# Hybrid encoder step: fewer and later kept weight pairs, norm stages apart, and other buffers and turns for column stores and loads

## The chip, the core and the metric

The kernel runs on one core of a Trainium2 chip. The metric is the device time in microseconds of one execution. Of the kernel before there are three such times: 2317.66, 2319.67 and 2321.96, median 2319.67. One further execution was profiled; every duration below is from it.

## The reference

One layer of a streaming encoder in float32, for 2048 prompt tokens and 32 sample tokens of width 1024:

```python
h = layer_norm(x, ln_in_g, ln_in_b)
z = einsum('btd,de->bte', h, w_in)              # 1024 -> 2304
ax, ag, bq, bk, bv, bg, cq, ck, cv = split(z)
o_a = rg_lru(causal_conv(ax)) * gelu(ag)        # A, 4 channel groups
o_b = head_norm(retention(bq, bk, bv)) * silu(bg)   # B, 4 heads
o_c = sliding_window_attention(cq, ck, cv)      # C, 8 query heads, 2 kv heads
m = einsum('bte,ed->btd', concat(o_a, o_b, o_c), w_out)
h = layer_norm(ALPHA * h + m, ln1_g, ln1_b)
f = einsum('btf,fd->btd', silu(h @ w_gate) * (h @ w_up), w_down)   # hidden width 2816
y = layer_norm(ALPHA * h + f, ln2_g, ln2_b)
```

Besides y, the new states of the three mixers are returned. float32 accuracy is reached with three matmuls for one product: weight and activation are each split into a high part (fp32r) and the rest, and high x high, rest x high and high x rest are added up.

## The kernel before

**Two halves.** The first half of the program takes the prompt in six blocks of 256, 384, 384, 384, 384 and 256 tokens; the 32 sample tokens go with block 0. It does LN, input projection, mixers, output projection and LN1 of all blocks, and the SwiGLU of block 0 in between. The second half, from 1093 us to the end, does the SwiGLU of the other 1792 tokens with combined (Strassen-like) products; its lines are 1330 and higher. The change is nearly all in the first half.

**Units.** The first half is a list of units, one for each weight tile of 0.5 MB. W units (18 in a block, f = 0 to 17) are the input projection, 24 matmuls each (L908, through `product`); O units (8 in a block) the output projection; G units (44, two for each f of 0 to 21) gate and up of block 0; D units its down projection. They run in this order: W of block 0, W of block 1, O of block 0, W of block 2, O of block 1, and so on to O of block 4; then G and D of block 0 up to f = 11, O of block 5 (the last), and G and D to f = 21. In the profiled execution, W of block 1 begins at about 105 us, W of the last block at about 701, and G at about 816.

**A unit's weights.** `feed` issues the load of a raw tile on SP's queue (L245, three `stage` buffers). `split` makes the pair from it: ScalarE writes the high part (L250), VectorE the rest (L254). The `pair` buffers are three. A unit that `keeps` names also stores its pair to DRAM (L261, two DMAs of 512 KB, in `keptW` or `keptO`); in later blocks `known` is true, and the finished pair (1 MB) is loaded (L238) with no split. Units of odd x are kept in block 1, those of even x in block 2.

**What sets the order.** The program writes the order of every engine's instructions out itself. Ahead of each unit's matmuls come `feed`, `split`, `run_late` (actions that were put off by one unit) and `step`. `step` is one turn: it advances side work written as generators. Those in `express` go on by a fixed number of yields; the others take turns while `pace["credit"]` lasts, which grows with the unit's time and falls by the cost that each yield names. `wait(n)` yields for n turns. An engine works through its instructions in order, so an instruction that waits holds up all behind it on its engine, and an engine's DMA queue likewise.

**Side work that the change touches.**
- `norm` (n for LN, m for LN1 of a block): per row tile the statistics (L372 to L374), then two passes (L380, L382) on VectorE; `pipeline` runs the tiles a stage apart. One norm at a time: its name stands in the list `norming`.
- `gained` (g0): multiplies block 0's three row tiles by the LN gain and adds its offset (six passes, L398) in block 1's W units. It puts "g0" into `norming` too.
- `mix_b` (B): retention in chunks; L716 to L725 states and statistics, L731 normalises into `b_o`, L737 transposes it on TensorE, L739 writes it out.
- `to_memory` (in m): TensorE transposes the LN1 output (L429), ScalarE copies it from PSUM to one of three `stg` buffers (L431) and stores it from its own queue to DRAM (L433 for block 0, L439 for others).
- `columns0` (f0): loads block 0's columns back in three parts (L470) and splits them (L473, L474) for the G units.
- `columns_first` (x0): in the last G units loads the first columns of the second half (L1273, L1277) and makes their sums and splits (L1289 to L1297). It is started by `change`, once m of the last block is drained.
- G units make `g_t` (L964, L965, L972), its high part `hCh` (L973) and the rest `hCl` (L978); D units (`t_unit`, L995 to L1005) add up in PSUM banks taken from the four `mm` banks, and `accumulate` adds these to the rows (L1022, L1026).

Of the kernel before, what the change touches and what calls it, by code (L numbers as in the profile page):

```python
# [97 lines left out]
def tile_hybrid_step(ctx: ExitStack, tc: tile.TileContext, io, outs):  # L98
# [117 lines left out]
    def keeps(u):  # L216

        kind, b, x = plan[u][:3]
        return kind in "WO" and b == 1 + (x % 2 == 0)

    def known(u):

        kind, b, x = plan[u][:3]
        return kind in "WO" and b > 1 + (x % 2 == 0)

    def unit_pair(u):
        pair = fw.tile([128, 2048], F32R, name="pair", bufs=NUNIT)
# [61 lines left out]
    def step():  # L289

        for name, n in list(express.items()):
            for _ in range(n):
                if name in side:
                    advance(name)
        pace["turns"] += 1
        pace["credit"] = min(pace["credit"], pace["most"]) + pace["rate"]
        for name in pace["turn"][:]:
            if pace["credit"] <= 0.0:
                break
            pace["turn"].remove(name)  # L300
            pace["turn"].append(name)
            pace["credit"] -= advance(name)

    def wait(turns):

# [51 lines left out]
    def norm(name, b, g, be):  # L357

        while norming or len(tok.get(b, ())) < len(ttiles(b)) or pace["turns"] < arrived.get(b, 0):
            yield 0.0  # L360
        norming.append(name)
        n = len(ttiles(b))
        gt, bt = bcast(g), bcast(be)
        here = pace["turns"] + 4
        st = sb.tile([128, n, 2, 6], F32, name="ln_st", bufs=2)
        mv = sb.tile([128, n, 2], F32, name="ln_mv", bufs=2)
        rs = sb.tile([128, n], F32, name="ln_rs", bufs=2)

        def tile_(t, rows):
            x = tok[b][t][:rows, :]  # L370
            for i in range(2):
                dve.bn_stats(st[:rows, t, i, :], x[:, i * 512:(i + 1) * 512])  # L372
            dve.bn_aggr(mv[:rows, t, :], st[:rows, t])
            dve.tensor_scalar(rs[:rows, t:t + 1], mv[:rows, t, 1:2], EPS, None, op0=ALU.add)  # L374
            yield 1.75
            pool.tensor_tensor(rs[:rows, t:t + 1], rs[:rows, t:t + 1], mhalf[:rows, 0:1], op=ALU.pow)
            yield 0.1
            while pace["turns"] < here:
                yield 0.0
            dve.scalar_tensor_tensor(x, x, mv[:rows, t, 0:1], gt[:rows, :], op0=ALU.subtract, op1=ALU.mult)  # L380
            yield 1.35
            dve.scalar_tensor_tensor(x, x, rs[:rows, t:t + 1], bt[:rows, :], op0=ALU.mult, op1=ALU.add)  # L382
            yield 1.35

        yield from pipeline([tile_(t, rows) for t, (_, rows) in enumerate(ttiles(b))], 1)
        norming.clear()

    def gained(b):
# [33 lines left out]

    def to_memory(b):

        def half(t, c0, rows, h):
            p = sdbank().rearrange("p (f c) -> p f c", f=4)
            for f in range(4):
                ft = 4 * h + f
                pe.transpose(p[:, f, :rows], tok[b][t][:rows, ft * 128:(ft + 1) * 128], ident[:rows, :rows])  # L429
            stg = sb.tile([128, 4, 128], F32, name="stg", bufs=3)  # L430
            act.activation(stg[:, :, :rows], p[:, :, :rows], AF.Copy)  # L431
            if b == 0:
                act.dma_start(cols0[:, 4 * h:4 * h + 4, c0:c0 + rows], stg[:, :, :rows])  # L433
            else:
                s, off = divmod(START[b] + c0 - START[NBLK], PART)
                for th in range(2):
                    a0, a1 = max(off, th * HALF), min(off + 128, th * HALF + HALF)
                    if a0 < a1:
                        act.dma_start(cols1[s, th, h][:, :, a0 - th * HALF:a1 - th * HALF],  # L439
                                     stg[:, :, a0 - off:a1 - off])  # L440
            yield 0.1

        yield from pipeline([half(t, c0, rows, h) for t, (c0, rows) in enumerate(ttiles(b)) for h in range(2)], 2)
# [20 lines left out]
    def columns0():  # L464

        h, l = hB[0] = hl(0, "hA")
        n = ncol(0)
        for k0, k1 in ((0, 3), (3, 6), (6, 8)):
            w = row_tile()[:, :(k1 - k0) * n].rearrange("p (k c) -> p k c", c=n)
            sp.dma_start(w, cols0[:, k0:k1, :])  # L470
            yield from wait(4)
            for k in range(k0, k1):
                act.activation(h[:, k, :], w[:, k - k0, :], AF.Copy)  # L473
                dve.tensor_tensor(l[:, k, :], w[:, k - k0, :], h[:, k, :].bitcast(F32), op=ALU.subtract)  # L474
                yield 0.5
# [189 lines left out]
    def mix_b(b):  # L665
# [11 lines left out]
        def chunk(c0, n, state, gi):  # L677
# [54 lines left out]
                                  op0=ALU.subtract, op1=ALU.mult)  # L732
            yield 1.4
            yield 0.0
            pt = sdbank().rearrange("p (f c) -> p f c", f=4)
            for i in range(2):
                pe.transpose(pt[:, i, :n], on[:n, 2 * i:2 * i + 2, :].rearrange("p h e -> p (h e)"), ident[:n, :n])  # L737
# [245 lines left out]
    def t_unit(b, key, kts, wh, wl, wf, first, last):  # L983

        tiles = ttiles(b)
        if first:
            banks[key] = [mmbank() for _ in tiles]
        wh, wl, wf = (w if w is None else w.rearrange("p (k c) -> p k c", k=2) for w in (wh, wl, wf))
        for x, (ah, al, _) in enumerate(kts):
            for t, (c0, rows) in enumerate(tiles):  # L990
                if rows < 128:
                    continue
                o = banks[key][t]
                cs = slice(c0, c0 + rows)
                pe.matmul(o, ah[:, cs], wh[:, x, :], start=first and x == 0, stop=False)  # L995
                pe.matmul(o, al[:, cs], wh[:, x, :], start=False, stop=False)  # L996
                pe.matmul(o, ah[:, cs], wl[:, x, :], start=False, stop=last and x == 1)  # L997
            if x == 0 and pace["twice"]:
                step()
        if tiles[-1][1] < 128:  # L1000

            for x, (_, _, a) in enumerate(kts):
                for h in range(2):
                    q = 2 * h + x
                    pe.matmul(banks[key][-1][32 * q:32 * q + 32, 0:256], a, wf[:, x, h * 256:(h + 1) * 256],  # L1005
                              start=first, stop=last)
# [261 lines left out]

    def columns_first():

        a = [two(), two()]
        for k in range(2):
            sp.dma_start(a[k], cols1[0, 0, 0][:, 2 * k:2 * k + 2, :])  # L1273
# [111 lines left out]

    kept_pair = {}

    def new_pair(key):
        at, n = (wp, 3) if clock["made"] % NPAIR < 3 else (sb, NPAIR - 3)
        clock["made"] += 1  # L1390
        pair = at.tile([128, 2, 512], F32R, name="pair", bufs=n)
# [29 lines left out]
    def w_keep(key):  # L1421

        def fn():
            sums[key[1:]] = dr.tile([128, 2, 512], F32, name="sum%d%s" % key[1:])
            sp.dma_start(sums[key[1:]], kept_pair[key].bitcast(F32))
        jobs.append(("store", fn, ()))

    def w_known(key):
# [79 lines left out]

    def background(n):
        clock["slot"] += 1  # L1510
        loads()
        while n and clock["done"] < clock["next"]:
            kind, _, on = jobs[clock["done"]]
# [403 lines left out]
```

## Time and profile before

| | us |
|---|---|
| median of three executions | 2319.67 |
| the profiled execution | 2317.79 |
| its span | 2315.8 |

ScalarE's waits in the first half show where the side work stands in the way of others: L250 waited for `stage` loads 58.7 us in 16 waits (in_wgu), 38.0 in 9 (in_wout) and 33.2 in 12 (in_win), all beside running matmuls but a few. One DMA queue moves 407.35 of the 417.90 MB. The profile is read from the span's start; a row of the timeline has start, duration, engine, line, operation, tiles (out<-in), and in brackets the idle time before it with what ended it.

### The profile page before, as it was taken

The numbers are of one execution on the slowest core, as the hardware profiler recorded it, in microseconds if no ns is written. First come the engines' busy times: TensorE is split into PE (matmuls) and PEld (weight loads), VectorE is DVE, ScalarE is ACT, GpSimd is POOL, SyncE is SP. The second block draws the span as 40 slices with busy tenths as digits, with TensorE's granted clock in tenths as the row PEclk, the third lists the DMA queues.
The fourth block names the chain that finished last, engine by engine and source line by source line (L and its number), as shares of the span: only waits on it lengthen the run. The fifth ranks groups of instructions, "written<-read, shape, count | busy, mean of one in ns | idle before, by whom it ended". The sixth has DMA issues, their size and how long they took to land.

```text
span 2315.8 us, 31921 instructions
## 1 busy us (share of the span) xinstructions
PE 2243.0 (97%) x12168; PEld 1956.8 (84%) x12168; DVE 1479.7 (64%) x2656; ACT 790.6 (34%) x1585; POOL 158.0 (7%) x236
## 2 busy tenths in 40 slices
PE   8999999999999999989999999999999999999996
PEld 7887888988888879877888988888888888898884
DVE  7795757566446375567876766677787544454557
ACT  5646263351523334234322332322331222232221
POOL 2010201101001011010000000000000000000004
PEclk9999999999999999989999999999999999999998
DMA  6563686767758765764643442433556343343341
GB/s 221 177 197 111 233 268 212 273 225 244 265 184 309 263 199 174 254 210 146 248 158 115 159 151 95 168 127 130 203 187 215 122 154 114 110 154 115 132 132 64
DMA packets 139272, 417.90 MB, mean 180 GB/s; under 512 B 20272, under 2 KB 35440, under 8 KB 127472
## 3 DMA queue, kind: packets, MB, share of 16 engines
q1 hardware_dynamic: 119056, 407.35, 51.4%
q10 hardware_dynamic: 20064, 8.52, 1.3%
q8 instruction: 96, 1.57, 0.3%
q14 instruction: 56, 0.46, 0.1%
HBM read 316.55 MB, written 99.26 MB: 180 GB/s over the span
## 4 chain that ended last, share of the span: by engine, by line
PE 25%; issue 22%; DVE 3%; DMA 1%; POOL 0%; ACT 0%; SPq 0%; DVEq 0%; ACTq 0%; POOLq 0%
PE gu L1578 16%; PE mm L1647 3%; PE mm L1646 3%; PE mm L1648 3%; DVE end_st L1713 0%; DVE tok L1711 0%; DVE end_mv L1721 0%; POOL end_rs L1718 0%; DMA pair<-sum3t 0%; DVE pair L1406 0%; DMA out_y<-tok 0%; DVE xl L1330 0%; DVE tok L1733 0%; DMA tok<-rows 0%; DVE tok L1333 0%
## 5 line engine op out<-in xcount | busy, mean ns | idle before, releaser
L1578 PE MATMUL gu<-xh,pair 128*128 128x448 f32 x2464 | 555.4, 367 | 7.1 <-DVE two L1600 2.9
L1578 PEld LDWEIGHTS gu<-xh,pair 128*128 128x128 f32 x2464 | 463.5, 188 | 50.0 <-issue 3.7
L908 PE MATMUL mm<-hAh,pair 128*128 128x384 f32 (+2 forms) x2432 | 424.6, 323 | 16.4 <-DVE pair L254 5.6
L908 PEld LDWEIGHTS mm<-hAh,pair 128*128 128x128 f32 x2432 | 376.6, 192 | 40.9 <-issue 17.7
L1401 ACT ACTIVATE pair<-ww 128x512 fp32r<-128x512 f32 x308 | 189.8, 626 | 515.8 <-PE mm L1648 237.9
L1578 PE MATMUL gu<-xl,pair 128*128 128x448 f32 x1232 | 303.0, 367 | 0.1
L1406 DVE TENSOR_TENSOR pair<-ww,pair 128x512 fp32r<-128x512 f32 x308 | 208.4, 688 | 147.9 <-ACT pair L1401 137.8
L1578 PEld LDWEIGHTS gu<-xl,pair 128*128 128x128 f32 x1232 | 232.1, 189 | 21.4 <-DVE xl L1330 1.1
L1655 DVE TENSOR_TENSOR tok<-tok,mm 128x512 f32<-128x512 f32 x181 | 124.1, 688 | 161.2 <-PE mm L1648 160.2
L1646 PE MATMUL mm<-pair,g 128*128 128x512 f32 x571 | 225.1, 394 | 1.8 <-DVE tok L1653 1.8
L1647 PE MATMUL mm<-pair,g 128*128 128x512 f32 x571 | 225.1, 394 | 0.0
L1648 PE MATMUL mm<-pair,g 128*128 128x512 f32 x571 | 224.6, 393 | 0.0
L908 PE MATMUL mm<-hAl,pair 128*128 128x384 f32 (+2 forms) x1216 | 211.2, 316 | 0.0
L250 ACT ACTIVATE pair<-stage 128x1024 fp32r<-128x1024 f32 x131 | 138.1, 1055 | 189.1 <-DMA stage<-in_wgu 58.7
L908 PEld LDWEIGHTS mm<-hAl,pair 128*128 128x128 f32 x1216 | 192.5, 192 | 0.0
L254 DVE TENSOR_TENSOR pair<-stage,pair 128x1024 fp32r<-128x1024 f32 x130 | 158.2, 1218 | 31.1 <-ACT pair L250 28.7
L1646 PEld LDWEIGHTS mm<-pair,g 128*128 128x128 f32 x571 | 107.3, 188 | 27.1 <-DVE tok L1653 2.3
L1648 PEld LDWEIGHTS mm<-pair,g 128*128 128x128 f32 x571 | 107.4, 188 | 24.9
L1647 PEld LDWEIGHTS mm<-pair,g 128*128 128x128 f32 x571 | 107.3, 188 | 24.3
L995 PE MATMUL mm<-pair,hCh 128*128 128x512 f32 x216 | 91.1, 422 | 7.3 <-DVE tok L1026 4.7
L997 PE MATMUL mm<-pair,hCh 128*128 128x512 f32 x216 | 86.7, 401 | 0.5 <-DVE pair L254 0.4
L996 PE MATMUL mm<-pair,hCl 128*128 128x512 f32 x216 | 86.9, 402 | 0.2 <-DVE hCl L978 0.2
(297 smaller groups left out, 2641.4 us busy)
## 6 DMA issues: line engine op xcount, KB each, us to landing
pair<-keptW SPq DMA_DIRECT2D x63, 1024.0 KB, 5.4
ww<-in_wgu SPq DMA_DIRECT2D x154, 256.0 KB, 3.2
pair<-keptO SPq DMA_DIRECT2D x28, 1024.0 KB, 4.9
stage<-in_win SPq DMA_DIRECT2D x45, 512.0 KB, 4.7
stage<-in_wgu SPq DMA_DIRECT2D x44, 512.0 KB, 4.2
ww<-in_wdn SPq DMA_DIRECT2D x88, 256.0 KB, 3.1
keptW<-pair SPq DMA_DIRECT2D x36, 512.0 KB, 8.0
stage<-in_wdn SPq DMA_DIRECT2D x22, 512.0 KB, 3.8
```

What stands on the lines that cost most here:

```text
L250: act.activation(whi[u], staged[u], AF.Copy)
L254: eng.tensor_tensor(wlo[u], staged[u], whi[u].bitcast(F32), op=ALU.subtract)
L908: pe.matmul(p, w[:, k, :], a[:, k, :], start=(x == 0 and k == 0), stop=(x == 2 and k == 7))
L995: pe.matmul(o, ah[:, cs], wh[:, x, :], start=first and x == 0, stop=False)
L996: pe.matmul(o, al[:, cs], wh[:, x, :], start=False, stop=False)
L1401: act.activation(pairs[key][1], whole_w[x], AF.Copy)
L1406: dve.tensor_tensor(pairs[key][0], whole_w[x], pairs[key][1].bitcast(F32), op=ALU.subtract)
L1578: pe.matmul(bank[n], w[:, k * 128:k * 128 + 128], a[:, k, :], start=first and x == 0 and k == 0, stop=x == 2 and k == 3, skip_group_check= ...
L1646: pe.matmul(bank, gh, wh, start=first and f == fs[0], stop=False)
L1647: pe.matmul(bank, gl, wh, start=False, stop=False)
L1648: pe.matmul(bank, gh, wl, start=False, stop=last and f == fs[-1])
L1655: dve.tensor_tensor(r, r, bank, op=ALU.add)
```

## The change

It does eight things.
1. `keeps`, `known`: odd x are kept in block 1, x%4 = 2 in block 2, x%4 = 0 in block 3; in the last block even x are loaded raw and split again.
2. `norm` runs its pipeline with each stage as a yield of its own, and `step` then goes on with what is in `norming` while credit is left. This holds for g0 as well.
3. `to_memory` of the last block uses halves of row tiles in place of the three `stg` buffers.
4. `columns0` loads one part ahead.
5. `mix_b` has one more yield ahead of its transposes.
6. `t_unit` takes the `gu` banks of the second half for the D units of half 1, once these exist.
7. `columns_first` waits six turns first.
8. The second half's stores of kept sums are put off by one turn.

```diff
--- before.py
+++ after.py
@@ -216,12 +216,14 @@
     def keeps(u):
 
         kind, b, x = plan[u][:3]
-        return kind in "WO" and b == 1 + (x % 2 == 0)
+        return kind in "WO" and b == 1 + (x % 2 == 0) + (x % 4 == 0)
 
     def known(u):
 
         kind, b, x = plan[u][:3]
-        return kind in "WO" and b > 1 + (x % 2 == 0)
+        if b == NBLK - 1 and x % 2 == 0:
+            return False
+        return kind in "WO" and b > 1 + (x % 2 == 0) + (x % 4 == 0)
 
     def unit_pair(u):
         pair = fw.tile([128, 2048], F32R, name="pair", bufs=NUNIT)
@@ -300,6 +302,12 @@
             pace["turn"].remove(name)
             pace["turn"].append(name)
             pace["credit"] -= advance(name)
+        for name in [n for n in pace["turn"] if n in norming]:
+            while name in side and name in norming and pace["credit"] > 0.0:
+                cost = advance(name)
+                pace["credit"] -= cost
+                if cost < 0.5:
+                    break
 
     def wait(turns):
 
@@ -382,7 +390,7 @@
             dve.scalar_tensor_tensor(x, x, rs[:rows, t:t + 1], bt[:rows, :], op0=ALU.mult, op1=ALU.add)
             yield 1.35
 
-        yield from pipeline([tile_(t, rows) for t, (_, rows) in enumerate(ttiles(b))], 1)
+        yield from pipeline([tile_(t, rows) for t, (_, rows) in enumerate(ttiles(b))], 1, True)
         norming.clear()
 
     def gained(b):
@@ -422,12 +430,19 @@
 
     def to_memory(b):
 
+        spare = {}
+
         def half(t, c0, rows, h):
             p = sdbank().rearrange("p (f c) -> p f c", f=4)
             for f in range(4):
                 ft = 4 * h + f
                 pe.transpose(p[:, f, :rows], tok[b][t][:rows, ft * 128:(ft + 1) * 128], ident[:rows, :rows])
-            stg = sb.tile([128, 4, 128], F32, name="stg", bufs=3)
+            if b < NBLK - 1:
+                stg = sb.tile([128, 4, 128], F32, name="stg", bufs=3)
+            else:
+                if h == 0:
+                    spare[t] = row_tile().rearrange("p (h f c) -> p h f c", h=2, f=4)
+                stg = spare[t][:, h]
             act.activation(stg[:, :, :rows], p[:, :, :rows], AF.Copy)
             if b == 0:
                 act.dma_start(cols0[:, 4 * h:4 * h + 4, c0:c0 + rows], stg[:, :, :rows])
@@ -465,10 +480,18 @@
 
         h, l = hB[0] = hl(0, "hA")
         n = ncol(0)
-        for k0, k1 in ((0, 3), (3, 6), (6, 8)):
+
+        def load(k0, k1):
             w = row_tile()[:, :(k1 - k0) * n].rearrange("p (k c) -> p k c", c=n)
             sp.dma_start(w, cols0[:, k0:k1, :])
-            yield from wait(4)
+            return w
+
+        ks_ = ((0, 3), (3, 6), (6, 8))
+        ahead = load(*ks_[0])
+        yield from wait(6)
+        for i, (k0, k1) in enumerate(ks_):
+            w = ahead
+            ahead = load(*ks_[i + 1]) if i < 2 else None
             for k in range(k0, k1):
                 act.activation(h[:, k, :], w[:, k - k0, :], AF.Copy)
                 dve.tensor_tensor(l[:, k, :], w[:, k - k0, :], h[:, k, :].bitcast(F32), op=ALU.subtract)
@@ -732,6 +755,7 @@
                                   op0=ALU.subtract, op1=ALU.mult)
             yield 1.4
             yield 0.0
+            yield 0.0
             pt = sdbank().rearrange("p (f c) -> p f c", f=4)
             for i in range(2):
                 pe.transpose(pt[:, i, :n], on[:n, 2 * i:2 * i + 2, :].rearrange("p h e -> p (h e)"), ident[:n, :n])
@@ -984,7 +1008,7 @@
 
         tiles = ttiles(b)
         if first:
-            banks[key] = [mmbank() for _ in tiles]
+            banks[key] = [gbank("xzyv"[t], 512) if pg and key == ("D", 1) else mmbank() for t in range(len(tiles))]
         wh, wl, wf = (w if w is None else w.rearrange("p (k c) -> p k c", k=2) for w in (wh, wl, wf))
         for x, (ah, al, _) in enumerate(kts):
             for t, (c0, rows) in enumerate(tiles):
@@ -1268,6 +1292,7 @@
 
     def columns_first():
 
+        yield from wait(6)
         a = [two(), two()]
         for k in range(2):
             sp.dma_start(a[k], cols1[0, 0, 0][:, 2 * k:2 * k + 2, :])
@@ -1385,7 +1410,16 @@
 
     kept_pair = {}
 
+    stores = []
+
+    def store_kept():
+
+        for d, x in stores:
+            sp.dma_start(d, x)
+        stores.clear()
+
     def new_pair(key):
+        store_kept()
         at, n = (wp, 3) if clock["made"] % NPAIR < 3 else (sb, NPAIR - 3)
         clock["made"] += 1
         pair = at.tile([128, 2, 512], F32R, name="pair", bufs=n)
@@ -1421,8 +1455,8 @@
     def w_keep(key):
 
         def fn():
-            sums[key[1:]] = dr.tile([128, 2, 512], F32, name="sum%d%s" % key[1:])
-            sp.dma_start(sums[key[1:]], kept_pair[key].bitcast(F32))
+            d = sums[key[1:]] = dr.tile([128, 2, 512], F32, name="sum%d%s" % key[1:])
+            stores.append((d, kept_pair[key].bitcast(F32)))
         jobs.append(("store", fn, ()))
 
     def w_known(key):
@@ -1508,6 +1542,7 @@
 
     def background(n):
         clock["slot"] += 1
+        store_kept()
         loads()
         while n and clock["done"] < clock["next"]:
             kind, _, on = jobs[clock["done"]]
```

The order of instructions shows what this moves. First VectorE in the W units of block 1, where g0 runs. Before (L398 is `gained`, L731 and L739 are `mix_b`, L254 a unit's split):

```order
L691 TENSOR_TENSOR b_k<-sd,tb 128x256
L699 TENSOR_TENSOR b_s<-sd,tb 128x2x128 x2
L398 TENSOR_TENSOR tok<-tok 128x1024
L731 TENSOR_SCALAR b_o<-sd,b_mv,b_rs 128x64 x4
L398 TENSOR_TENSOR tok<-tok 128x1024
L254 TENSOR_TENSOR pair<-stage,pair 128x1024
```

The same place in the changed kernel, where these lines are L714, L722, L406, L754 and L256:

```order
L714 TENSOR_TENSOR b_k<-sd,tb 128x256
L722 TENSOR_TENSOR b_s<-sd,tb 128x2x128 x2
L406 TENSOR_TENSOR tok<-tok 128x1024 x2
L406 TENSOR_TENSOR tok<-tok 32x1024
L406 TENSOR_TENSOR tok<-tok 128x1024
L754 TENSOR_SCALAR b_o<-sd,b_mv,b_rs 128x64 x4
L406 TENSOR_TENSOR tok<-tok 128x1024
L406 TENSOR_TENSOR tok<-tok 32x1024
L256 TENSOR_TENSOR pair<-stage,pair 128x1024
```

All six passes of g0 now stand ahead of one split; before, two stood ahead of it, and the other four ahead of the next two. Next, SP's queue where f0 loads block 0's columns, in O of block 4. Before:

```order
L470 DMA tok<-cols_83 128x864
L238 DMA pair<-keptO_5429 128x2048
L238 DMA pair<-keptO_4062 128x2048
L245 DMA stage<-in_wgu 128x1024 x4
L470 DMA tok<-cols_83 128x576
L168 DMA tok<-rows_0_2956 128x1024
```

In the changed kernel (L486, L240, L247):

```order
L486 DMA tok<-cols_83 128x864
L240 DMA pair<-keptO_5429 128x2048
L486 DMA tok<-cols_83 128x576
L240 DMA pair<-keptO_4051 128x2048
L247 DMA stage<-in_wgu 128x1024 x4
L168 DMA tok<-rows_0_2950 128x1024
```

The third load of columns moved ahead of one kept pair and the first four raw tiles of the G units. Last, VectorE in the G units of f = 17, where x0's sums stand. Before:

```order
L965 SCALAR_TENSOR_TENSOR g_t<-g_t,mm 128x288
L254 TENSOR_TENSOR pair<-stage,pair 128x1024
L1296 TENSOR_TENSOR two<-two 128x896
L1297 TENSOR_TENSOR g<-g,two 128x896
L1289 TENSOR_TENSOR xl<-two,xh 128x896
L972 SCALAR_TENSOR_TENSOR g_t<-g_t,mm 128x288
L254 TENSOR_TENSOR pair<-stage,pair 128x1024
```

In the changed kernel (L989, L256, L1317, L996 for L965, L254, L1292, L972):

```order
L989 SCALAR_TENSOR_TENSOR g_t<-g_t,mm 128x288
L256 TENSOR_TENSOR pair<-stage,pair 128x1024
L1317 TENSOR_TENSOR g<-two,g 128x896
L996 SCALAR_TENSOR_TENSOR g_t<-g_t,mm 128x288
L256 TENSOR_TENSOR pair<-stage,pair 128x1024
```

Ahead of the row that makes g_t, three of x0's instructions became one; the other sums moved to the units of f = 18 to 21.

## The prediction

> **What bounds the kernel now.** First the page's head, then the table of windows over both halves and over four stretches of 50 us: it says which engine is full, and where it is not.
>
> ```profile
> span 2315.8 us, 31921 instructions
> PE 2243.0 (97%) x12168; PEld 1956.8 (84%) x12168; DVE 1479.7 (64%) x2656; ACT 790.6 (34%) x1585; POOL 158.0 (7%) x236
> ...
> 0.00:1093.00 1093.00, 1052.47 (x6615) 912.18 (x6615) 698.76 (x1447) 452.39 (x992) 126.90 (x205) 0.98 0.65 221
> 1093.00:2315.80 1222.80, 1190.55 (x5561) 1044.57 (x5553) 780.90 (x1210) 338.25 (x593) 31.09 (x31) 0.99 0.43 145
> ...
> 250.00:300.00 50.00, 49.82 (x310) 46.90 (x308) 33.52 (x73) 14.05 (x30) 10.90 (x13) 1.00 0.88 311
> 700.00:750.00 50.00, 46.73 (x376) 43.69 (x375) 33.16 (x79) 18.11 (x57) 6.52 (x16) 0.97 0.89 318
> 950.00:1000.00 50.00, 44.75 (x260) 40.35 (x259) 23.13 (x33) 13.95 (x19) 4.69 (x5) 0.95 0.80 278
> 1000.00:1050.00 50.00, 46.98 (x286) 37.51 (x285) 38.14 (x54) 18.48 (x23) 3.59 (x3) 0.92 0.56 200
> ```
>
> A window's columns are its length, the busy time of PE, PEld, DVE, ACT and POOL, PEclk, the share of the DMA engines and GB/s. TensorE is busy for 97% and does the same matmuls after the change, so all that can be won is its idle time, 2315.8 - 2243.0 = 72.8 us, and the time it runs on a halved clock. In the first half that is 1093.0 - 1052.5 = 40.5 us. Busy DMA alone costs nothing: 250 to 300 moves 311 GB/s with PE at 49.82 of 50. So the next view is PE's waits, by what ended them.
>
> ```profile
> PE mm L908 <- DVE pair L254: 5.6, 5, 2.3
> PE mm L908 <- ACT pair L250: 4.9, 1, 4.9
> PE mm L995 <- DVE tok L1026: 4.7, 1, 4.7
> PE sd L813 <- ACT stg L431: 3.5, 2, 2.2
> ...
> PE mm L908 <- DMA pair<-keptW: 2.8, 2, 1.7
> ...
> PE mm L995 <- ACT hCh L973: 2.7, 1, 2.7
> ...
> PE mm L908 <- ACT hAh L473: 2.1, 1, 2.1
> ...
> PE sd L737 <- DVE b_o L731: 1.7, 2, 1.5
> ```
>
> Columns: total us, times, longest. These 28.0 us are what the edits aim at; each is one or a few stalls. The last view is the granted clock just behind them.
>
> ```profile
> 41.00:47.00 6.00, 3.90 (x29) 3.90 (x30) 5.86 (x14) 0.47 (x2) 0.00 (x0) 1.00 0.42 115
> ...
> 731.00:737.00 6.00, 5.76 (x37) 5.76 (x37) 0.60 (x3) 2.59 (x10) 0.25 (x2) 0.72 0.93 354
> 818.00:825.00 7.00, 6.22 (x34) 6.07 (x35) 6.14 (x14) 3.70 (x7) 0.67 (x1) 0.76 0.84 297
> ...
> 996.10:1003.00 6.90, 6.90 (x34) 6.90 (x35) 4.03 (x7) 2.98 (x5) 1.07 (x1) 0.62 0.77 258
> 1036.60:1044.00 7.40, 7.16 (x24) 4.41 (x25) 6.06 (x11) 1.72 (x2) 1.03 (x1) 0.61 0.20 69
> ```
>
> A stall can cost twice: the clock lost behind it is 0.28 x 6 = 1.7 us at 731, 0.24 x 7 = 1.7 at 818, 0.38 x 6.9 = 2.6 at 996 and 0.39 x 7.4 = 2.9 at 1036; none at 41, where PE had just idled 2.29 us. The Trainium skill, "TensorE: Matmul & The Clock Gate", section on the HAM clock gate, says that the clock is halved after at least one idle window of about 3.4 us. The trace disagrees: at 731 the longest wait was 1.7 us, and the clock fell. By the rule only the 4.9 and the 4.7 us stall would carry a clock term: of the gains below some 7 us would go, and of the losses the 1.7 in block 1, so the time would be about 2308; I go by the rows.
>
> **The change part by part.**
>
> *Kept weights.* Units with odd x are kept in block 1, those with x%4 = 2 in block 2, with x%4 = 0 in block 3, and the last block splits even x anew. Reloads fall from 63 + 28 to 71, so 20 units are loaded raw and split again.
>
> ```profile
> pair<-keptW SPq DMA_DIRECT2D x63, 1024.0 KB, 5.4
> ...
> pair<-keptO SPq DMA_DIRECT2D x28, 1024.0 KB, 4.9
> ...
> L250 ACT ACTIVATE pair<-stage 128x1024 fp32r<-128x1024 f32 x131 | 138.1, 1055 | 189.1 <-DMA stage<-in_wgu 58.7
> ...
> L254 DVE TENSOR_TENSOR pair<-stage,pair 128x1024 fp32r<-128x1024 f32 x130 | 158.2, 1218 | 31.1 <-ACT pair L250 28.7
> ```
>
> That is +20 x 1.055 = 21 us of ACT and +20 x 1.218 = 24.4 us of DVE, 13 of the 20 in the last block (9 W, 4 O), 7 in block 3. From 700 to 750 DVE is busy 33.16 of 50 us; 376 matmuls at 24 a unit are at most 15 W units, so at most 8 more splits, 9.7 us, which makes 43 of 50: hidden on average. It removes both waits for keptW (2.8) and the clock behind one (1.7): bound +4.5. Against it stands the block's start:
>
> ```profile
> 110.00:166.00 56.00, 52.83 (x338) 47.35 (x338) 53.91 (x125) 21.72 (x52) 13.14 (x19) 1.00 0.67 214
> ...
> 701.00:718.00 17.00, 15.90 (x131) 15.67 (x132) 16.57 (x39) 1.93 (x5) 5.23 (x9) 1.00 0.92 354
> ```
>
> DVE is full there (16.57 of 17), and two more splits, 2.4 us, can come out on PE, with a clock drop of 1.7 at worst. I take **+2.5** (-2 to +4.5).
>
> Near 300, the store of a kept pair goes out ahead of the next stage load:
>
> ```profile
> 291.32 0.95 SPq L261 DMA_DIRECT2D keptW<-pair  x2
> ...
> 304.33 0.59 PE L813 MATMUL sd<-kb,zq 64*128 64x192 f32 x2 [2.25 <-ACT stg L431]
> ```
>
> It is the store of an even unit with x%4 = 0, which block 2 no longer makes. The stage arrives sooner, ACT's L250 is early, and with it the L431 that PE waited for (3.5, and 1.7 of clock, priced as at 731, the nearest row): bound +5.2, taken **+4** (0 to 5.2).
>
> *Norm stages.* norm yields per stage, and step() then advances whatever is in `norming` while credit is left. Block 0's wait at 43.10 (2.3 of the 5.6 on L254) should go, with about 1 left a few units on: **+1.5** (0 to 2.8). But `gained` puts "g0" into `norming`, so its six multiplies and adds are all pumped into block 1's first units. DVE before:
>
> ```profile
> 116.09 1.22 DVE L254 TENSOR_TENSOR pair<-stage,pair 128x1024 fp32r<-128x1024 f32 x1
> ...
> 120.78 1.20 DVE L398 TENSOR_TENSOR tok<-tok 32x1024 f32<-32x1024 f32 x1
> ...
> 122.93 1.20 DVE L398 TENSOR_TENSOR tok<-tok 128x1024 f32<-128x1024 f32 x1
> 124.06 1.21 DVE L254 TENSOR_TENSOR pair<-stage,pair 128x1024 fp32r<-128x1024 f32 x1
> ```
>
> Two L398 stand ahead of each of these splits; now all six stand ahead of the first: 4 x 1.2 = 4.8 us more. DVE is busy 53.91 of 56 us here, so there is no slack to repay it from: the split that ended at 117.3 ends near 122, and adding up DVE's rows between the later splits, norm's stages included, gives the next units 1.3, 4, 6 and 5 us late. Two stalls that stood here, for L731 (1.7) and for zv, are inside that. 5 us late plus a clock drop of 1.7 (as at 731): **-6.5** (-9 with a second drop and a third stall; +2.6 if DVE's total alone counts and both old stalls go).
>
> *Last block's columns.* The fourth copy of to_memory waited until a stg buffer was stored; in row buffers it waits for none.
>
> ```profile
> 993.78 0.60 ACT L431 ACTIVATE stg<-sd 128x512 f32<-128x512 f32 x1 [4.85 <-DMA cols<-stg]
> ...
> 996.09 4.21 PE L908 MATMUL mm<-hAh,pair 128*128 128x288 f32 x16 [4.93 <-ACT pair L250]
> ```
>
> The L250 behind it comes about 4 us sooner; the four copies with their issues (1.2 us each) still stand ahead of it, so 1 to 1.5 of the stall may stay. Stall and clock 4.93 + 2.6 = 7.5: **+6** (4 to 7.5).
>
> *columns0 ahead.* SP's third column load was queued behind four stage loads:
>
> ```profile
> 801.55 12.62 SPq L245 DMA_DIRECT2D stage<-in_wgu  x4
> ...
> 818.28 0.78 ACT L473 ACTIVATE hAh<-tok 128x288 fp32r<-128x288 f32 x2 [5.65 <-DMA tok<-cols]
> ```
>
> It now stands ahead of them. Stall 2.15 and clock 1.7 go: **+3.85** (3 to 3.85); the four stage loads were spread over 12.62 us by their own buffers, and one issue ahead of them is hidden in that.
>
> *columns_first six turns later.* Three column sums stood ahead of L972, whose hCh PE waited for:
>
> ```profile
> 1032.60 1.08 DVE L1296 TENSOR_TENSOR two<-two 128x896 f32<-128x896 f32 x1
> ...
> 1035.61 0.44 DVE L972 SCALAR_TENSOR_TENSOR g_t<-g_t,mm 128x288 f32<-128x288 f32 x1
> ```
>
> Only one (1.08 us) stands there now, so 2.2 us of DVE leave: stall 2.7 and clock 2.9 make 5.6, taken **+4.5** (2 to 5.6). The sums come at units that had none: **-0.5** (-2 to 0).
>
> *D's second half in gu banks.* Its first matmul at 1084 no longer waits for L1026 to empty a bank (4.7). But DVE's L254, which the next matmuls need, comes after that L1026 anyway:
>
> ```profile
> 1086.30 1.21 DVE L254 TENSOR_TENSOR pair<-stage,pair 128x1024 fp32r<-128x1024 f32 x1
> ```
>
> It ends at 1087.5, so most of the wait changes its name: **+1** (0 to 3).
>
> *mix_b a turn later* and *stores of kept sums*: +0.3 and **0**. In the order of instructions SP's queue in the second half reads as before, the sum stores included, and so do the other engines; 1222.8 us of the span stay.
>
> The **sum** is 2.5 + 4 + 1.5 - 6.5 + 6 + 3.85 + 4.5 - 0.5 + 1 + 0.3 = 16.65 us. The profiled execution took 2317.79, 2 us beyond its span; 2317.79 - 16.65 = 2301.1. The median shown, 2319.67, is 1.9 above the profiled run: forecast **2303**.
>
> **Rivals.**
> - *All covers hold, and the pumping costs nothing.* The terms at +2.6 instead of -6.5 and +2.5 of the kept and stg bounds give 16.65 + 9.1 + 2.0 + 1.2 = 29: 2291. For it: norm's total work is the same. Against it: DVE at 53.91 of 56.
> - *The stalls only change their releaser.* Only the 3.85 and half of 6 + 4.5 stay, less 6.5: +2.6, so 2317: the same. For it: the L1026 case above.
> - *Slower: VectorE becomes the bound.* The 20 added L254 come bunched behind norm stages, in units where DVE has no gap. It decides from where DVE's work between two L254 passes two units of PE: in block 1 that is so already (53.91 of 56), in the last block it is at most 43 of 50, but full at its start. If all 24.4 us come out on PE, with 9 of block 1, against the 23.15 of the sum without its -6.5: 2319.67 + 10.25 = 2330.
> - *An edit does nothing*: the sum stores; it is in the sum at nothing.
>
> **How the numbers follow.** Forecast (2297 to 2311) 0.57, the first rival 0.18, the second 0.15, the third 0.10. The range takes the forecast, most of the first rival and the better part of the second: 2289 to 2316. 0.2%, about what a measurement of this kernel can tell from no change, is 4.6 us, so faster ends at 2315.0: faster 0.82, same 0.11, slower 0.07.
>
> **What would show it.** After: no PE wait for keptW, hAh or stg; the wait for L250 near 996 under 1.5 us; L254 x150 and L250 x151; in 110 to 166 us PE stalls on L254 and L731 of some 6 us, with PEclk under 1; from 1093 on the same 1222.8 us. Wrong would be: no loss in block 1 (then 2296 or less), or new waits on L254 in 700 to 800 of over 5 us (then the third rival).

## The result, and the profile after

The changed kernel takes 2307.56 us (median of four executions, 2306.0 to 2308.54). The kernel before, run again beside it, takes 2320.82 (four, 2317.66 to 2322.71). The ratio is 0.9944, with a 95% interval of 0.9926 to 0.9961: 13.3 us between the medians. The profiled executions are 9.4 us apart (2317.79 and 2308.36). Forecast were 2303 and a range of 2289 to 2316.

The page of the changed kernel, and its waits of TensorE (total us, times, longest):

```profile
span 2306.6 us, 31976 instructions
...
PE 2237.1 (97%) x12168; PEld 1951.0 (85%) x12168; DVE 1500.4 (65%) x2676; ACT 811.7 (35%) x1605; POOL 171.4 (7%) x236
```
```profile
PE sd L721 <- DVE b_k L714: 6.8, 2, 5.5
PE mm L932 <- DVE pair L256: 4.9, 8, 1.1
PE gu L1021 <- DVE pair L256: 3.9, 2, 3.4
...
PE sd L837 <- ACT c_pt L873: 2.3, 1, 2.3
...
PE mm L932 <- DMA pair<-keptW: 1.8, 1, 1.8
PE sd L837 <- ACT stg L446: 1.8, 2, 1.4
...
PE mm L932 <- ACT pair L252: 1.5, 1, 1.5
...
PE mm L1019 <- ACT hCh L997: 0.6, 1, 0.6
```

ScalarE is 21.1 us busier, just what 20 added L250 cost, and VectorE 20.7, a little under the 24.4 of 20 splits. The single wait for L250 fell from 4.9 to 1.5, that for hCh from 2.7 to 0.6, that for hAh at 818 is gone. But three entries are new or larger: b_k (5.5 in one wait), c_pt, and the split L256 (L254 before) ahead of D's matmuls in the gu banks.

Totals don't say where the time went, so the timeline is cut into stages. Each begins with the first matmul of a block's W units, of the G units of f = 0, 12 or 18, or of the second half, and lasts to the next; what is put between (O units, mixers, D units) is in the stage it falls in. Durations in us, from TensorE's timeline of the profiled executions:

| stage | before | after | won | forecast |
|---|---|---|---|---|
| W of block 0 | 82.94 | 80.46 | 2.5 | 1.5 |
| W of block 1 | 155.18 | 162.33 | -7.2 | -6.5 |
| W of blocks 2 to 4 | 447.86 | 441.25 | 6.6 | 4 + 0.3 |
| W of the last block | 114.72 | 123.21 | -8.5 | 2.5 |
| G of f 0 to 11 | 153.55 | 148.03 | 5.5 | 3.85 |
| G of f 12 to 17 | 76.05 | 65.82 | 10.2 | 6 + 4.5 |
| G of f 18 to 21 | 48.06 | 48.01 | 0.05 | 1 - 0.5 |

The gains add up to 9.2 us; the forecast's terms add up to 16.65. Blocks 2 to 4 stand in one row because some work moved between them. The second half took 1205.5 us before (its first to the last matmul) and 1205.6 after: it kept its time, as forecast. One line is off by 11 us, the last block's; the others lie within 2.5.

A stage varies between executions even where its instructions are the same. Five profiled executions here run block 0 as the kernel before does (that kernel, and e6 to e9 below); its W units took 82.90 to 85.52 us, those of block 1 154.18 to 155.18, those of blocks 2 to 4 446.66 to 449.70. G of f 12 to 17 took 73.94 to 76.58 in the four executions with neither edit 3 nor edit 7 (the kernel before, e8, e9, e10), and 65.82 to 70.14 in the eight with both. So a difference of 2 to 3 us in one row of one execution is not much more than this scatter, and the 10.2 of f 12 to 17 is the best of eight.

**Block 1** lost where it was expected. The row of the window of 110 to 166 us, then VectorE and TensorE around the stall:

```profile
110.00:166.00 56.00, 47.91 (x292) 42.87 (x292) 48.99 (x108) 19.96 (x48) 20.08 (x19) 0.91 0.53 181
```
```profile
110.68 4.75 DVE L406 TENSOR_TENSOR tok<-tok 128x1024 f32<-128x1024 f32 x4
115.36 1.08 DVE L754 TENSOR_SCALAR b_o<-sd,b_mv,b_rs 128x64 f32<-128x64 f32 x4
116.37 2.34 DVE L406 TENSOR_TENSOR tok<-tok 128x1024 f32<-128x1024 f32 x2
118.64 1.20 DVE L256 TENSOR_TENSOR pair<-stage,pair 128x1024 fp32r<-128x1024 f32 x1
...
122.09 0.41 DVE L714 TENSOR_TENSOR b_k<-sd,tb 32x256 f32<-32x256 f32 x1
```
```profile
122.55 0.42 PE L721 MATMUL sd<-zb 64*32 64x32 f32 x4 [5.48 <-DVE b_k L714]
122.89 5.46 PE L932 MATMUL mm<-hAh,pair 128*128 128x384 f32 x16
...
131.59 3.05 PE L932 MATMUL mm<-hAh,pair 128*128 128x384 f32 x16
```

The six passes of g0 (7.1 us) stand in two lumps ahead of the next chunk's b_k, and TensorE's scores (L721) wait for that: one stall of 5.48, and 16 matmuls behind it take 5.46 us, where the same 16 of the next unit take 3.05. The granted clock (the column before the last two) says why:

```profile
117.90:128.20 10.30, 5.65 (x21) 5.59 (x22) 10.04 (x33) 0.00 (x0) 1.57 (x2) 0.50 0.43 154
```

The prediction had the split end near 122 and the wait on it; it ended at 119.84, and the wait fell on b_k, which stands a few rows further on.

**The last block** lost where a small gain was expected. TensorE, ScalarE and SP's queue there:

```profile
733.27 1.22 PE L932 MATMUL mm<-hAh,pair 128*128 128x256 f32 x8 [1.82 <-DMA pair<-keptW]
...
736.37 0.91 PE L837 MATMUL sd<-kb,zq 64*128 64x192 f32 x4 [1.45 <-ACT stg L446]
739.63 1.64 PE L837 MATMUL sd<-kb,zq 64*128 64x192 f32 x4 [2.35 <-ACT c_pt L873]
```
```profile
721.45 1.06 ACT L252 ACTIVATE pair<-stage 128x1024 fp32r<-128x1024 f32 x1 [3.06 <-DMA stage<-in_win]
...
734.78 1.06 ACT L252 ACTIVATE pair<-stage 128x1024 fp32r<-128x1024 f32 x1 [5.10 <-DMA stage<-in_win]
735.74 0.58 ACT L446 ACTIVATE stg<-sd 128x512 f32<-128x512 f32 x1
```
```profile
723.22 0.34 SPq L809 DMA_DIRECT2D out_p_v<-c_v  x1
...
724.13 1.68 SPq L472 DMA_DIRECT2D rows<-tok  x3
725.90 1.14 SPq L240 DMA_DIRECT2D pair<-keptW  x1
727.09 1.20 SPq L247 DMA_DIRECT2D stage<-in_win  x1
```
```profile
SPq L809 <- ACT c_kst L813: 7.4, 1, 7.4
```

SP issues a raw tile only after what stands ahead of it in its queue. That is a kept pair, which waits for a pair buffer (from 700 to 816 us L240 waited 56.2 us in 11 waits for matmuls), and here also a store (L809) that waits 7.4 us for copies of ScalarE; these stand behind the split at 721.45, which had waited for its own raw tile. So the next raw tile is issued at 727.09 only. It lands 7.6 us later, and ScalarE, which works in order, stands in L252 for 5.1 us until then, with the copies for stg and the attention (L446, L846, L873) queued behind it. TensorE waits for these. VectorE is not full: in 718 to 816 us it is 43 of 98 us busy. Whether its added work costs something all the same is what e11 tests.

```profile
718.00:816.00 98.00, 90.28 (x600) 76.92 (x601) 43.28 (x103) 42.78 (x112) 5.10 (x12) 0.97 0.64 233
```

### The profile page after: what moved, and what is told of

It is laid out like the page before. It is cut to its first block, busy times and chain, and to the rows that moved or that the text cites. A ratio compares the mean times of both kernels' runs of the same rounds, so it can differ in the third digit from the quotient of the medians.

```text
span 2306.6 us, 31976 instructions
## 1 busy us (share of the span) xinstructions
PE 2237.1 (97%) x12168; PEld 1951.0 (85%) x12168; DVE 1500.4 (65%) x2676; ACT 811.7 (35%) x1605; POOL 171.4 (7%) x236
## 4 chain that ended last, share of the span: by engine, by line
PE 26%; issue 22%; DVE 2%; DMA 0%; POOL 0%; ACT 0%; SPq 0%; DVEq 0%; POOLq 0%; ACTq 0%
PE gu L1613 16%; PE mm L1682 3%; PE mm L1681 3%; PE mm L1683 3%; DVE end_st L1748 0%; DMA out_y<-tok 0%; DVE tok L1746 0%; DVE end_mv L1756 0%; POOL end_rs L1753 0%; DVE xl L1355 0%; DVE tok L1358 0%; DVE tok L1768 0%; DMA tok<-rows 0%; DVE pair L1440 0%; DVE tok L529 0%
## 5 line engine op out<-in xcount | busy, mean ns | idle before, releaser
L252 ACT ACTIVATE pair<-stage 128x1024 fp32r<-128x1024 f32 x151 | 159.5, 1057 | 234.0 <-DMA stage<-in_win 58.8
L256 DVE TENSOR_TENSOR pair<-stage,pair 128x1024 fp32r<-128x1024 f32 x150 | 183.3, 1222 | 41.7 <-ACT pair L252 41.7
L1019 PE MATMUL mm<-pair,hCh 128*128 128x512 f32 x196 | 80.8, 412 | 0.6 <-ACT hCh L997 0.6
L1021 PE MATMUL mm<-pair,hCh 128*128 128x512 f32 x196 | 77.6, 396 | 0.7 <-DVE pair L256 0.7
L1644 ACT ACTIVATE two<-two 128x448 f32<-128x448 f32 x44 | 25.5, 580 | 148.0 <-DVE two L1642 148.0
```

The lines of the kernel that those rows point to most:

```text
L252: act.activation(whi[u], staged[u], AF.Copy)
L256: eng.tensor_tensor(wlo[u], staged[u], whi[u].bitcast(F32), op=ALU.subtract)
```

## The experiments

The theory is that two parts of the change give back 7 and some 10 us: g0 in the added loop, and raw tiles in the last block through ScalarE's wait. Its rivals: VectorE's sum of work, or the DMA traffic, binds in both places. Four runs test these, four take one edit alone or back, two more do that for the rest, one repairs a flawed test, and the last joins the repairs.

### e1: g0 not pumped

```diff
-        for name in [n for n in pace["turn"] if n in norming]:
+        for name in [n for n in pace["turn"] if n in norming and n != "g0"]:
```

> The changed kernel, but step() no longer pumps g0; all else as changed. Theory (the six g0 passes bunched ahead of chunk 1's b_k are the loss in block 1): the 5.48 us wait for b_k at 122.55 goes, PEclk in 118 to 128 is 1.0 again, block 1 ends some 7 to 9 us sooner, the whole takes 2299 to 2301. Rival (VectorE's sum in block 1 binds in any order): the wait moves to another row of 110 to 166 us, the whole takes 2305 to 2308.

Measured: W of block 1 takes 156.18 us instead of 162.33. The waits there:

```profile
PE sd L721 <- DVE b_k L714: 3.7, 2, 2.3
```

So 6.2 of the 7.2 us come back, and g0's lumps are the cause; 2.3 us of wait for b_k and a short clock drop stay. The whole, however, takes 2305.98 (2304.19 to 2308.26), ratio to before 0.9949 (0.9934 to 0.9964), not 2300: 1.6 us under the changed kernel's median. In the profiled execution the second half begins 3.95 us sooner than in the changed kernel's, and ends 0.6 sooner: the second half, the same program, took 3.3 us more. Its clock differs, here at two places:

```profile
1685.20:1692.00 6.80, 6.29 (x17) 5.08 (x17) 6.76 (x9) 4.75 (x7) 0.00 (x0) 0.50 0.40 125
1767.10:1770.50 3.40, 3.40 (x8) 2.73 (x9) 3.40 (x5) 0.00 (x0) 0.00 (x0) 0.50 0.76 264
```

The same places in the changed kernel's execution:

```profile
1688.10:1691.50 3.40, 3.29 (x9) 2.62 (x9) 3.37 (x5) 1.96 (x3) 0.00 (x0) 0.50 0.00 0
1767.10:1770.50 3.40, 1.72 (x7) 1.43 (x8) 2.46 (x4) 0.00 (x0) 0.00 (x0) 1.00 0.87 324
```

e1 spent 10.2 us on half clock there and the changed kernel 3.4; half of the difference, 3.4 us, is about what the second half took longer. The edit doesn't touch the second half, which took 1204.9 to 1210.4 us over the eight profiled executions of the changed kernel and its variants. So the stages are compared, and not only the whole. What the other executions lost isn't known, since one of each kernel is profiled; the same edit on top of e3 (it makes e12) takes 5.7 us off the median.

### e2 and e3: the last block's raw tiles

e2 loads all of the last block's pairs as kept ones:

```diff
-        if b == NBLK - 1 and x % 2 == 0:
-            return False
```

> The changed kernel, but the last block loads all its pairs as kept ones; nothing there is split anew. Theory (raw tiles in the last block cost some 8 us net, because ScalarE stands in L252 until a late raw tile lands): the waits for stg and c_pt at 736 to 740 go, a wait for keptW of 2 to 3 us in all with a clock term of 1.7 stays or comes back, the whole takes 2301 to 2304. Rival (the spread of traffic is what gained there): keptW waits as before the change and more, the whole takes 2307 to 2310.

e3 keeps the splits and issues a raw tile of the last block ahead of the kept pair before it:

```diff
             if known(u):
+                v = u + 1
+                if (v < len(plan) and plan[v][1] == NBLK - 1 and plan[v][0] in "WO" and not known(v)
+                        and v not in staged and v < i + 6):
+                    live = [k for k in staged if not (k < i if raw(k) else k < front["lo"])]
+                    if len(live) < NSTAGE:
+                        staged[v] = fw.tile([128, 1024], F32, name="stage", bufs=NSTAGE)
+                        sp.dma_start(staged[v], plan[v][3])
                 if u >= i + NUNIT or front["lo"] < u:
                     break
...
-            else:
+            elif u not in staged:
```

> The changed kernel, but in the last block a raw tile is issued ahead of the kept pair before it, so one unit sooner; the splits stay. Theory (ScalarE waits for the late raw tile): its idle before L252 for in_win in 718 to 816 us falls from about 5 us a time to under 2, PE's waits at 736 to 740 go, the whole takes 2300 to 2303. Rival (the 13 added splits on VectorE are the cost): the same waits stay, the whole takes 2307.

Measured: W of the last block takes 112.73 us in e2 and 112.45 in e3, against 123.21. The whole takes 2303.12 (2301.22 to 2306.42; ratio 0.9938, 0.9923 to 0.9953) and 2298.56 (2298.12 to 2300.71; ratio 0.9918, 0.9904 to 0.9933). TensorE's waits in the last block, e2 first, then e3:

```profile
PE mm L930 <- DMA pair<-keptW: 2.2, 2, 1.5
...
```
```profile
PE mm L939 <- DMA pair<-keptW: 1.2, 1, 1.2
PE mm L939 <- DVE pair L263: 0.5, 1, 0.5
...
```

The longest waits of ScalarE in the same stretch, in the changed kernel and in e3:

```profile
ACT pair L252 <- DMA stage<-in_win: 18.9, 6, 5.1
```
```profile
ACT b_v L719 <- PE sd L718: 15.3, 2, 10.0
ACT pair L259 <- DMA stage<-in_wgu: 9.9, 1, 9.9
```

SP's queue in e3, where L816 is L809 of the changed kernel:

```profile
714.59 0.43 SPq L244 DMA_DIRECT2D stage<-in_win  x1
719.85 0.34 SPq L816 DMA_DIRECT2D out_p_v<-c_v  x1
```

This settles the cause. e3 has every split, raw tile and byte of the changed kernel, and only the raw tiles' place in SP's queue is other. The tile that was issued at 727.09 is now issued at 714.59, ahead of the store; ScalarE's six waits for in_win, 18.9 us, are gone, and 10.8 us come back. Neither VectorE's work nor the traffic was the cost.

### e4 and e11: the VectorE work of the splits by itself

Both reload the last block's pairs as e2, and add 13 VectorE operations as long as a split. e4's reads the pair whose load has just been issued (first diff, beside e2's edit); e11's reads a constant table (second diff):

```diff
+    def again(u):
+        s = fw.tile([128, 1024], F32, name="stage", bufs=NSTAGE)
+        dve.tensor_tensor(s, whi[u].bitcast(F32), wlo[u].bitcast(F32), op=ALU.add)
...
                 front["hi"] = front["lo"] = u + 1
+                if plan[u][1] == NBLK - 1 and plan[u][2] % 2 == 0:
+                    later(lambda u=u: again(u))
```
```diff
-        dve.tensor_tensor(s, whi[u].bitcast(F32), wlo[u].bitcast(F32), op=ALU.add)
+        dve.tensor_tensor(s, tb[:, 0:1024], tb[:, 512:1536], op=ALU.add)
```

> As e2, but each even pair of the last block is followed by one VectorE addition of its two parts into a stage buffer (128x1024, as long as a split; its result is not used): the VectorE work of the splits without ScalarE and raw tiles. Theory (ScalarE and the raw tile): within 2 us of e2. Rival (VectorE): 6 to 9 us above e2, near the changed kernel's time.

> As e4, but the added VectorE operation reads a constant table, so it waits for no load; 13 operations of 1.2 us in the last block. Theory (e4's loss was VectorE standing still for a load, not the work): W of the last block takes 113 to 115 us (112.73 in e2), no stall over 2 us near 700 or 750. Rival (the work itself): over 120.

e4 takes 2320.11 (2312.63 to 2323.87), 17 us more than e2, which looks like the rival's case. But the added operation had a wait of its own that the other kernels don't have; VectorE in e4:

```profile
748.06 1.23 DVE L233 TENSOR_TENSOR stage<-pair 128x1024 f32<-128x1024 f32 x1 [7.79 <-DMA pair<-keptW]
```

It stood 7.8 us for a pair that TensorE needs only later, with mixer work queued behind it. The first of the 13 stood 12.3 us at 693.56, ahead of the last block's first matmul, and W of blocks 2 to 4 took 451.74 us, against 441.34 in e2. So e4 doesn't test the work. e11 does: W of the last block takes 112.48 us (112.73 in e2), the whole 2303.69 in one execution. The 13 operations cost nothing there.

### e5: kept weights as before

The rules of the kernel before for what is kept in which block; the last block's raw tiles stay as in the changed kernel:

```diff
-        return kind in "WO" and b == 1 + (x % 2 == 0) + (x % 4 == 0)
+        return kind in "WO" and b == 1 + (x % 2 == 0)
...
-        return kind in "WO" and b > 1 + (x % 2 == 0) + (x % 4 == 0)
+        return kind in "WO" and b > 1 + (x % 2 == 0)
```

> The changed kernel, but with the kept weights of the kernel before: all even x kept in block 2, all reloaded in the last block. Theory (spread stores are what removed the waits near 301 and 304): a wait for stg of 2 to 3.5 us comes back there, W of blocks 2 to 4 take 445 to 448 us (441.3 as changed, 447.9 before), and the last block takes 112 to 115 us as in e2. Rival (norm's stages and the later transposes removed them): blocks 2 to 4 stay at 441 to 442 us, and the whole takes 2299 to 2302.

The expectation's words on the last block don't fit this kernel, since that clause stayed; its last block took 123.53 us, as in the changed kernel. Blocks 2 to 4 took 451.05 us (441.25 with the change), with these waits, which the changed kernel has only as one of 0.3:

```profile
PE sd L837 <- ACT stg L446: 4.0, 2, 2.3
PE sd L721 <- DVE b_k L714: 2.3, 1, 2.3
```

SP's queue shows how, from the start of block 2's W units to 312 us, in e5 and in the changed kernel:

```profile
SPq L240 <- DMA keptW<-pair: 37.4, 5, 10.1
```
```profile
SPq L240 <- DMA keptW<-pair: 16.3, 3, 9.1
```

A kept pair's load waits until the store out of its buffer has landed, and the raw tile stands behind that load. With fewer stores in block 2 this wait falls by 21 us. So the later keeping wins 9.8 us under the new norm order, more than the scatter of this stage; the whole took 2323.35, one execution.

### e6 to e10: one edit alone, on the kernel before

Each is the kernel before with one part of the diff above: e6 the row buffers in `to_memory`, e7 `wait(6)` in `columns_first`, e8 the gu banks in `t_unit`, e9 the load ahead in `columns0`, e10 the pipeline apart and the loop in `step`. One execution each beside a single profile, so the stages are read.

> The kernel before with one edit: the last block's to_memory in halves of row tiles. Theory: ScalarE's wait for cols<-stg (4.85) goes, the 4.93 us stall near 996 shrinks to 1 to 1.5 and its clock drop goes, G of f 12 to 17 takes 69 to 71 us instead of 76.05; the whole 2311 to 2314. Rival: the stall changes its releaser (L250 late for its own tile, or a row tile not free), 75 us or more.

> The kernel before with one edit: columns_first waits six turns. Theory: the 2.65 us stall for hCh near 1036 and the clock drop behind it go, G of f 12 to 17 takes 70 to 72 us; 0.5 to 2 us come back in f 18 to 21. Rival: the sums hold up another unit's L972 and the stall moves, 75 us or more. The stall near 996 stays in both.

> The kernel before with one edit: the D units of half 1 use gu banks. Theory: the 4.66 us wait for L1026 at 1084 turns into a wait for the split L254 of 3 to 4 us; G of f 18 to 21 with its D units gains 0.5 to 2 us of 48.06. Rival: the wait goes as a whole, 4 us or more.

> The kernel before with one edit: columns0 loads one part ahead. Theory: the 2.15 us wait for hAh at 818 and its clock drop go, G of f 0 to 11 takes 149 to 150 us instead of 153.55; the waits near 834 and 840 stay. Rival (another DMA lands last): the wait stays or turns into one for a stage tile, 152 us or more.

> The kernel before with one edit: norm's stages apart and the added loop in step(), g0 included. Theory (both the gain in block 0 and the loss in block 1 are this edit's): W of block 0 takes 80 to 81 us (82.94 before), W of block 1 161 to 163 (155.18), blocks 2 to 4 the same 448 as before within 2. Rival (the norm edit also removed the waits of blocks 2 to 4): these take 441 to 444.

| run | whole | stage | before | alone |
|---|---|---|---|---|
| e6 | 2319.03 | G of f 12 to 17 | 76.05 | 73.14 |
| e7 | 2314.93 | G of f 12 to 17 | 76.05 | 71.30 |
| e8 | 2320.15 | G of f 18 to 21 | 48.06 | 48.17 |
| e9 | 2315.66 | G of f 0 to 11 | 153.55 | 150.39 |
| e10 | 2320.47 | W of block 0 | 82.94 | 80.54 |
| e10 | | W of block 1 | 155.18 | 160.31 |
| e10 | | W of blocks 2 to 4 | 447.86 | 450.83 |

e6 gains 2.9 us, not 5 to 7. ScalarE shows what is left of the wait:

```profile
992.08 0.60 ACT L438 ACTIVATE tok<-sd 128x512 f32<-128x512 f32 x1 [0.90 <-ACT tok L438]
992.71 1.68 ACTq L446 DMA_DIRECT2D cols<-tok  x1
994.44 1.06 ACT L250 ACTIVATE pair<-stage 128x1024 fp32r<-128x1024 f32 x1 [1.76 <-issue]
```

The fourth copy no longer waits, but its DMA issue holds ScalarE for 1.68 us, and 2.08 us of TensorE's stall stay with a clock drop. That the stall fell from 4.93 to 2.08 is clear; a stage of 73.14 is only 0.8 under the lowest without the edit. e7 gains 4.75 there, where the stall for hCh falls from 2.65 to 0.82 and the clock drop behind it goes. The 0.85 that it gives back in f 18 to 21 lies within the scatter: e10, without that edit, took 49.10. e8 changes nothing: the wait for L1026 turns into one for the split.

```profile
PE gu L997 <- DVE pair L254: 4.7, 2, 4.5
```

e9 gains 3.2 (the four executions with the old loads and the old norm took 152.28 to 153.55), and the waits near 834 and 840 stay as expected. The changed kernel has G of f 0 to 11 at 148.03: its wait of 1.97 us at 840 is one of 1.1, without a clock drop. Which edit does that wasn't tried; e10 alone, at 150.59, shows that it is partly norm's.

e10 confirms that block 0's gain and most of block 1's loss are norm's and step's (5.1 of 7.2 us), and that norm wins nothing in blocks 2 to 4: its 450.83 is 1.1 above the highest without the edit. In block 1 its longest wait stands on another row than the changed kernel's:

```profile
PE sd L743 <- DVE b_o L737: 4.5, 3, 3.0
```

There g0's first lump (4.61 us from 109.71) stands right ahead of b_o. So the lumps are behind both waits, and which row they hold up depends on the other edits. The other 2.0 us of block 1 are open; the later transposes of `mix_b` weren't tried alone.

### e12: both repairs

The edits of e1 and e3 together.

> The changed kernel with both repairs: g0 not pumped, and raw tiles of the last block issued a unit sooner. If the two losses are apart from each other: W of block 1 156 us, W of the last block 112.5, the whole 2293 to 2296. If one only makes room for the other's wait: 2298 or more.

It takes 2292.9 us (median of six, 2291.25 to 2295.74), ratio to before 0.9893 (0.9876 to 0.9910). W of block 1 takes 154.41, W of the last block 110.94. The losses are apart from each other, and both can be had back: 25.2 us under the kernel before in the same runs (2318.06), in place of 13.3.

## Why the prediction was right, and where it was not

**The whole** came within 4.6 us of the forecast, inside the range, and faster by more than 0.2%. That it came so near is partly luck. On the profiled pair 9.4 us were won where the terms said 16.65; where the other 3.9 of the medians' 13.3 were won, no profile shows. One term was wrong in sign by 11 us and hid behind smaller errors the other way.

**The signs** that the prediction named: 150 and 151 splits came, and the loss in block 1 with it. But a wait for keptW (1.8 us) and two for stg (1.8) stayed that were to go. And the loss in the last block came without the sign that was to announce it, a wait of over 5 us on VectorE's split in 700 to 800.

**The failed step** is the kept weights' "+2.5 (-2 to +4.5)". It set the 20 splits' durations against the share of time in which VectorE and ScalarE were busy ("hidden on average"), and named VectorE at the block's start as the risk. The step left out what ScalarE's instruction waits for. A raw tile in a block of kept pairs is issued behind whatever SP's queue stands for, and ScalarE then stands in line for the tile. Ahead of 1.06 us of work it stood 5.1 us, and the term measured -8.5. The prediction had this very chain in its paragraph on 300 us (late tile, late L250, late L431, waiting TensorE) and didn't ask for it in the last block. e2 and e3 show the cause; e11 shows that the average was right for VectorE.

**Near 300**, right in mechanism (e5), and larger than +4: blocks 2 to 4 won 6.6 net, 9.8 against the old rules under the new norm order. Part of it came at a place that the prediction didn't name: e5's wait for b_k (2.3) is at 531 us, in O of block 2.

**g0 in block 1**, right in cause (e1) and about right in size, -7.2 for -6.5; the wait stood on b_k and not on the split. e10 has 5.1 for the edit that the term was made for, so the nearness of 7.2 is in part luck.

**The row buffers and the later first columns**: 10.2 for 10.5 together, which is the best of eight executions. Alone they give 2.9 and 4.75 (e6, e7), 7.65 in all. The 2.6 more need be no effect of having both: the stall left near 994 (1.50 us) had no clock drop behind it in the profiled execution of the changed kernel, and the same stall in e3 (1.52) had one, in a stage of 69.00 us. The row buffers were overrated, since 2.08 us and a clock drop stay in e6.

**columns0 ahead**: 3.2 alone for 3.85, right. **Block 0**: 2.5 for 1.5. **The gu banks**: +1 was 0. That the wait changes its name was said; the 1 us that it was to win wasn't there. The 3.43 us that stay:

```profile
1078.51 1.21 DVE L256 TENSOR_TENSOR pair<-stage,pair 128x1024 fp32r<-128x1024 f32 x1
...
1079.77 0.50 PE L1021 MATMUL gu<-pair,hCh 128*128 128x512 f32 x1 [3.43 <-DVE pair L256]
```

**Stores of kept sums**: 0, as the order of instructions said; the second half kept its time to 0.1 us, though it varied by 5.5 us over the executions of one program.

**The clock.** That short stalls cost clock was right again. The row of the last block behind the waits of 1.45 and 2.35 us:

```profile
739.20:746.00 6.80, 6.37 (x26) 4.95 (x26) 4.12 (x10) 3.06 (x9) 0.05 (x1) 0.50 0.18 44
```

In the 3.4 us ahead of that drop (735.8 to 739.2) TensorE still worked for 0.91 us. The rule of the Trainium skill ("TensorE: Matmul & The Clock Gate", section on the HAM clock gate), that it takes an idle window of about 3.4 us, isn't what this trace shows. That the time by the rule (2308) lay nearer to 2307.56 says nothing for it, since the last block's term alone was off by 11 us.

**The rivals.** That all covers hold did not come true; e12, with two repairs, comes to 2292.9, near the time of that rival (2291). That stalls only change their releaser came true for the gu banks alone. VectorE as the bound did not: e11 puts its price in the last block at nothing.

## What to carry to other kernels

Before work is moved from one engine to another, look at what its first instruction waits for, and what is queued behind it: a 1 us copy that waits 5 us for a load holds the whole queue, and an average busy share can't show it. Issue such a load ahead of anything on its own queue that can be held up, by a buffer or by another engine; here that place in a queue was worth 10.8 us. A rule that hurries one kind of side work (norm) should be looked at for everything that it catches (g0). And cut the timeline into stages, but learn each stage's scatter from executions in which its instructions are the same. W of block 0 took 80.41 to 80.54 us in the nine profiled executions with the new norm, and 82.90 to 85.52 in the five with the old. Whole times of one kernel spread over 2.5 to 15 us.

## What was not expected of the hardware

The clock after a short stall is not the same from one execution to the next. The stall for hCh near 1036 was 2.65 us in the kernel before, in e8 and in e9, with the same instructions there. Behind it the granted clock in 1036.6 to 1044 us was 0.61 in the kernel before and 0.58 in e8; in e9 it was whole:

```profile
1036.60:1044.00 7.40, 6.87 (x43) 4.63 (x43) 6.53 (x11) 2.24 (x3) 0.66 (x1) 1.00 0.26 75
```

G of f 12 to 17 took 76.05, 76.58 and 73.94 us in the three. Likewise the stall of 1.52 us at 983.00 in e3 was followed by 3.4 us of half clock, and the one of 1.50 at 993.77 in the changed kernel by none. The stretches on half clock quoted here last 3.4, 6.8 or 10.2 us, one, two or three of the same length. A stall of about 2 us thus costs its own length, or some 1.7 to 3.4 more (half of 3.4 to 6.8, an estimate). In e1's second half such stretches took back over half of what the edit had won in block 1.
